# A four-layer hybrid backbone: start-up reordered around the modulation steps, and the latent half of x loaded and squared later

## The chip, the cores and the metric

The kernel runs on one core of one Trainium2 chip. The metric is the time of one execution on the device in microseconds (us), the median of several runs. A core has five engines that run their own instruction streams and wait for one another by semaphores: TensorE (PE; its weight loads are listed as PEld), VectorE (DVE), ScalarE (ACT), GpSimd (POOL) and SyncE (SP), which issues most of the transfers. TensorE's granted clock has two levels, 1.2 and 2.4 GHz; the profile gives it as a share of the higher one.

## What is computed

Four layers run over 512 tokens of 1024 features: 256 context tokens and 256 latent tokens. Each layer has a mixer (latent attention in layers 0 and 3, a convolution module in layer 1, a Hyena operator in layer 2) and a gated feed-forward part with a short convolution. Each mixer and feed-forward part sees a normed and modulated input. Cut to what this case touches, in the reference:

```python
def rmsnorm(x, g):
    xf = x.astype(F32)
    y = xf * lax.rsqrt(jnp.mean(xf * xf, axis=-1, keepdims=True) + EPS)
    return (y * g.astype(F32)).astype(x.dtype)

def modulate(x, g, shift, scale):
    return rmsnorm(x, g) * (1 + scale) + shift
...
    sh1, sc1, g1, sh2, sc2, g2 = jnp.split(s_lat @ ada_w[i] + ada_b[i], 6, axis=-1)
    csh1, csc1, cg1, csh2, csc2, cg2 = jnp.split(s_ctx @ ada_w[i] + ada_b[i], 6, axis=-1)
    hl = modulate(x, norm_mix[i], sh1, sc1)
...
    hdn = jnp.sin(fr * (z @ f_w1.astype(F32) + f_b1.astype(F32)))
    hdn = jnp.sin(fr * (hdn @ f_w2.astype(F32) + f_b2.astype(F32)))
    hf = hdn @ f_w3.astype(F32)
...
    k = jnp.concatenate([h_fwd, jnp.zeros((1, D_MODEL), F32), h_bwd[1:][::-1]], axis=0)
    return k / (jnp.sum(jnp.abs(k), axis=0, keepdims=True) + EPS)
```

The modulation vectors come from `c` and `c_ctx` alone, and the spectrum of the Hyena filter from weights alone. The kernel computes both while it starts up, before and between the first products of layer 0.

## The kernel before

Features lie on the 128 partitions, in eight k-tiles; tokens lie along the free dimension, context in columns 0 to 255 and latent in 256 to 511. An fp32 number is split into a high and a low part (a ScalarE copy gives `whi`, `hh` or `g`, a VectorE subtraction gives `wlo`, `hl` or the second `g`), and a product is three matmuls (`mm3`, lines 158 to 160; two loops of line 636 and 642 in the attention's compression). In the trace an fp32 matmul stands as two entries.

The order of TensorE's instructions is that of the program text (`tc.manual_schedule(engines={PE})`). The order on the other engines is made by a scheduler; each engine then runs its list strictly in order. Transfers are issued from SP, one after the other, and an issue waits until its buffer is free.

The start-up, at the end of the program (lines 1360 to 1391), puts these together by hand:

- `warm_up(n)` (line 218) issues `n` matmuls of `ones` and `ident` whose result nobody uses (`idle` in the profile).
- `fill` takes the next step of `ada_group` (line 230): one k-tile of the first modulation vectors, four matmuls (`ada`, line 243). After the eighth, ScalarE copies the result out (line 248), and `settle` (line 254) transposes it and VectorE adds the bias (`mod`, line 262).
- `piece` takes the next step of the Hyena filter's spectrum: `spectra` (two sine layers on VectorE and ScalarE, lines 1100 to 1107, with four products between, line 1151), then `spectra_half(0, ...)` (line 1161). That makes for two halves `t` two products with the decay window (lines 1171, 1173, 1174), sum and difference, their splits, and the sum of absolute values `asum`; then four columns of spectra products (`fcol`, six matmuls each, copied out by line 1195), two to a piece.
- `Sq` (line 325) squares x on ScalarE (line 335) and adds the squares up (line 337); here on VectorE and over all 512 columns, six additions. `sums` (line 353) sums over the partitions with matmuls against `ones` (line 357), and ScalarE, a power on GpSimd (line 195) and ScalarE (line 364) make the token scales; `spread` (line 366) spreads them over the partitions by a matmul. `apply` (line 370) makes `moda` from `mod`, then for eight k-tiles `e` (VectorE), `hh` (ScalarE) and `hl` (VectorE). `apply(0)` is for the context, `apply(1)` for the latent tokens.
- `mla` (line 581) loads the compression weights `w_c` in two pairs (each split in two), and multiplies: for the context eight k-steps of line 636, with `sums(1)` behind the fourth, and the low halves (line 642), with `apply(1)` (and so the second `spread`) behind the first eight of them; then the same for the latent tokens.

The same `spectra_half` runs once more with `hc` of 1, by the spare steps of layer 1's feed-forward part, some 880 to 960 us into the span.

Of the kernel before, what the change touches and what calls it, by code (L numbers as in the profile page):

```python
# [15 lines left out]
AF = mybir.ActivationFunctionType  # L16
ALU = mybir.AluOpType
AX = mybir.AxisListType

P = 128  # L20
D = 1024
KT = D // P
T = 512
L = 256
# [11 lines left out]
CW = QL + KVL + PE  # L36
# [20 lines left out]
def r(ap):  # L57
    return ap.bitcast(F32R)
# [25 lines left out]
def kernel(ctx: ExitStack, tc: tile.TileContext, xT, cT, cB, ada0, ada2, adaT1, adaT2, adaT3, prm, mlp, w_c, w_ug, w_o,  # L84
                         w_p1, w_p2, w_hi1, w_hi0, w_ho, w_fup, w_fd0, w_fd1, w_fd2, spec0, f_w3, decay, dft, c_dft, c_b, out,
                         layers=(0, 1, 2, 3), final=True):
# [18 lines left out]
    def e_tile(shape=None):  # L105
        return gp.tile(shape or [P, T], F32, tag="g", name="e")
# [55 lines left out]
    def both(t, f):  # L162
        return f(t[0]), f(t[1])

    def stt(o, a, s, b, op0, op1, **kw):
        nc.vector.scalar_tensor_tensor(out=o, in0=a, scalar=s, in1=b, op0=op0, op1=op1, **kw)  # L166

    def split(hi, lo, src):
        nc.scalar.activation(out=r(hi), in_=src, func=AF.Copy)  # L169
        nc.vector.tensor_tensor(out=r(lo), in0=src, in1=hi, op=ALU.subtract)  # L170

    def rsqrt_seed(eng, v, n, tag):
        y = sp.tile([P, n], F32, tag=tag + "y", name="rsy", bufs=2)
# [44 lines left out]
    def warm_up(n):  # L218
        idle = pm.tile([P, T], F32, tag="mm", name="idle")
        for i in range(n):  # L220
            nc.tensor.matmul(out=idle[:, 0:P], lhsT=ident, rhs=ones, start=True, stop=True)  # L221
# [8 lines left out]
    def ada_group(li, g, early=False):  # L230
        mod_tile(li)
        ps = pa.tile([P, T], F32, tag="ada", name="ada")
        for k in range(KT):
            if early and k in (2, 3, 4):
                raws = [wp.tile([P, 1024], F32, tag="w", name="aw", bufs=WB) for _ in range(2)]
            else:
                raws = [wp.tile([P, 2048], F32, tag="raw", name="raw", bufs=RAW)]
            n = 4 // len(raws)
            for i, raw in enumerate(raws):
                at = (4 * g + n * i) * T  # L240
                nc.sync.dma_start(out=raw, in_=(ada0, None, ada2)[li][k * P:(k + 1) * P, at:at + n * T])
            for c in range(4):
                nc.tensor.matmul(out=ps[32 * c:32 * c + 32, :], lhsT=spad[:, k, :], rhs=raws[c // n][:, c % n * T:(c % n + 1) * T],  # L243
                                 start=(k == 0), stop=(k == KT - 1))
            if k < KT - 1:
                yield
        sb = e_tile()
        nc.scalar.activation(out=sb, in_=ps, func=AF.Copy)
        late.append((li, g, sb))
        yield  # L250

    late = []

    def settle():
        if not late:
# [43 lines left out]
    def fill(n=1):  # L299
        for _ in range(n):  # L300
            settle()
            if units[0] < cap[0] and next(filler[0], 1) is None:
                units[0] += 1
# [14 lines left out]
    def need(n):  # L318
        while units[0] < n:
            was = units[0]  # L320
            fill()
            if units[0] == was:
                break

    class Sq:
        def __init__(self, c0, eng=nc.gpsimd):
            self.c0, self.acc, self.n, self.parts, self.eng = c0, None, [0, 0], {}, eng
# [18 lines left out]
    class Norm:  # L346
# [23 lines left out]
        def apply(self, s):  # L370
            if s not in self.R:
                self.spread(s)
            R = self.R[s]
            v = slice(s * L, (s + 1) * L)
            self.m = mods[self.li]
            if self.a is None:
                self.a = sp.tile([P, KT, 2], F32, tag="moda", name="moda")
                stt(self.a, self.m[:, self.c + 8:self.c + 16, :], 1.0, self.g.unsqueeze(2).to_broadcast([P, KT, 2]),
                    ALU.add, ALU.mult)
            hs = []  # L380
            shift = lambda k: self.m[:, self.c + k, s:s + 1]
            for k in range(KT):
                hs.append(e_tile()[:, v])
                stt(hs[k], x[:, k, v], self.a[:, k, s:s + 1], R[:, v], ALU.mult, ALU.mult)
                nc.scalar.activation(out=r(HH[:, k, v]), in_=hs[k], func=AF.Identity, bias=shift(k))
            with tc.high_priority(offset=-18 if s == 0 else 0):
                for k in range(KT):
                    stt(r(HL[:, k, v]), hs[k], shift(k), HH[:, k, v], ALU.add, ALU.subtract)
# [192 lines left out]
    def mla(li, nm):  # L581
# [4 lines left out]
        cps = [ps_mm() for _ in range(4)]  # L586
        w = []
        for u in range(2):
            w += [both(t, lambda a: a.rearrange("p (k c) -> p k c", k=2)) for t in load_w(w_c[j, u], 2 * CW, 2 * CW)]
        if li == layers[0]:  # L590
            spill()
        widths = ((0, QL), (QL, QL + KVL), (QL + KVL, CW))
# [568 lines left out]
    def spectra_half(hc, loaded):  # L1161
        w3, dec, raw = loaded
        fh, fl = [g_tile(), g_tile()], [g_tile(), g_tile()]
        for t in range(2):
            split(fh[t], fl[t], raw[:, t * T:(t + 1) * T])
        fwd = lambda t, a, b: (fh[t][:, a:b], fl[t][:, a:b])
        ab, asum = [], []
        for t in range(2):
            pf, pb = ps_mm(), ps_mm()
            for w, ps in ((0, pf), (1, pb)):  # L1170
                nc.tensor.matmul(out=ps, lhsT=h2[:, t * P:(t + 1) * P], rhs=w3[w][0:FO, :], start=True, stop=True)
            f, b, s, d = e_tile(), e_tile(), e_tile(), e_tile()
            nc.vector.tensor_tensor(out=f, in0=pf, in1=dec[t], op=ALU.mult)
            nc.vector.tensor_tensor(out=b, in0=pb, in1=dec[t], op=ALU.mult)
            if t == 0:
                nc.vector.memset(b[0:1, :], 0.0)
            nc.vector.tensor_tensor(out=s, in0=f, in1=b, op=ALU.add)
            nc.vector.tensor_tensor(out=d, in0=b, in1=f, op=ALU.subtract)
            hl4 = [g_tile() for _ in range(4)]
            split(hl4[0], hl4[1], s)  # L1180
            split(hl4[2], hl4[3], d)
            ab.append(((hl4[0], hl4[1]), (hl4[2], hl4[3])))
            stt(f, f, -1.0, f, ALU.mult, ALU.max)
            stt(b, b, -1.0, b, ALU.mult, ALU.max)
            nc.vector.tensor_tensor(out=f, in0=f, in1=b, op=ALU.add)
            asum.append(f)
            yield
        kf = [[e_tile(), e_tile()] for _ in range(2)]
        for fcol, w in ((0, 0), (1, 0), (2, 1), (3, 1)):
            ps = ps_mm()  # L1190
            for t in range(2):
                mm3(ps, fwd(t, fcol * P, (fcol + 1) * P), ab[t][w], t == 0, t == 1)
            f2, im = fcol % 2, fcol // 2
            for j in range(2):
                nc.scalar.activation(out=kf[j][f2][:, im * L:(im + 1) * L], in_=ps[:, j * L:(j + 1) * L], func=AF.Copy)
            if fcol % 2:
                yield
        ps = ps_mm()
        for t in range(2):
            mm3(ps[0:32, :], fwd(t, 2 * P, 2 * P + 32), ab[t][0], t == 0, t == 1)  # L1200
        for j in range(2):
            nc.scalar.activation(out=kf[j][0][0:1, L:T], in_=ps[0:1, j * L:(j + 1) * L], func=AF.Copy)
            for f2 in range(2):
                nc.sync.dma_start(out=kf_d[:, 2 * hc + j, f2 * T:(f2 + 1) * T], in_=kf[j][f2])
        nps = ps_tr()
        for c in range(4):
            for t in range(2):
                nc.tensor.matmul(out=nps[:, c:c + 1], lhsT=asum[t][:, c * P:(c + 1) * P], rhs=ones[:, 0:1],
                                 start=(t == 0), stop=(t == 1))
        v = slice(4 * hc, 4 * hc + 4)  # L1210
        nc.vector.tensor_scalar(out=rn[:, v], in0=nps[:, 0:4], scalar1=EPS, scalar2=None, op0=ALU.add)
        nc.vector.reciprocal(out=rn[:, v], in_=rn[:, v])
        yield
# [147 lines left out]

    with tc.manual_schedule(engines={mybir.EngineType.PE}):
        filler[0] = chain(ada_group(0, 0, True), ada_group(0, 1), ada_group(0, 2), ada_group(2, 0))
        la, lb = spectra_load()
        pieces = chain(spectra(la), spectra_half(0, lb))
        sq = Sq(0, nc.vector)
        nm = Norm(layers[0], 0, sq)
        def piece():
            kas.extend(next(pieces) or ())

        warm_up(WARM)
        fill(2)
        for k in (0, 4):
            nc.sync.dma_start(out=x[:, k:k + 4, :], in_=xT[:, k:k + 4, :])
        for k in range(KT):
            sq.add(k, 0, T)
        for i in range(3):
            piece()
        warm_up(12)
        fill()  # L1380
        for i in range(2):
            piece()
            warm_up(6)
            fill()
        nm.sums(0)
        fill(3)
        piece()
        settle()
        piece()
        nm.apply(0)  # L1390
        spare[0] = pieces

        for i, li in enumerate(layers):
            nm = (mla, conformer, hyena)[li % 3](li, nm)
            nm = ffn(li, nm)
# [164 lines left out]
```

## Time and profile before

| What | us |
|---|---|
| median of 3 runs | 2145.06 (2144.52 to 2145.59) |
| profiled execution, its own time | 2145.16 |
| its span, first to last instruction | 2143.3 |
| TensorE busy | 2096.1 (98%) |
| VectorE busy | 1557.3 (73%) |
| ScalarE busy | 1287.5 (60%) |
| GpSimd busy | 236.2 (11%) |

The mean granted clock of the span is 0.994. In the chain of work that ended last, 89% is TensorE, 4% VectorE, 3% ScalarE, 2% GpSimd, 1% transfers. The first fortieth of the span (0 to 54 us) is the one in which TensorE is busy 0.7 of the time; nearly all the others show 0.9 or more.

### The profile page before, as it was taken

To read this page: it belongs to the slowest core of one execution; us is meant where nothing else is said; L and a number is where in the kernel's file an instruction comes from. 1 tells how busy PE (TensorE), PEld (TensorE's weight loads), DVE (VectorE), ACT (ScalarE), POOL (GpSimd) and SP (SyncE) were. 2 spreads that over 40 slices of the span, in tenths; PEclk is the share of its full clock that TensorE was granted. 3 is DMA by queue.
4 is the path that set the end of the run, shared out by engine and by line. 5 is a ranking of instruction groups with operands and counts; after the bars stand their busy time and mean duration, and the time that the engine had idled before them with its cause. 6 is when DMAs were issued, how large, how long until landed. Compare 5 with 4: busy or idle time off the path is not lost.

```text
span 2143.3 us, 32063 instructions
## 1 busy us (share of the span) xinstructions
PE 2096.1 (98%) x12108; PEld 1801.3 (84%) x12108; DVE 1557.3 (73%) x2780; ACT 1287.5 (60%) x2774; POOL 236.2 (11%) x403
## 2 busy tenths in 40 slices
PE   7999999999999999999999999999999998899999
PEld 5767898888899979888888988898888888669999
DVE  5878368889756665768775689757979856976665
ACT  3788457778644465547654544456868745875453
POOL 0375200000020012000000200020000002621000
PEclk8999999999999999999999999999999999999999
DMA  8533135545432152444542322224545531114552
GB/s 316 211 131 139 60 118 179 214 177 200 173 128 84 59 205 81 155 150 163 196 171 85 114 85 93 99 79 158 210 182 196 197 113 50 58 46 171 180 189 85
DMA packets 48699, 305.39 MB, mean 142 GB/s; under 512 B 5536, under 2 KB 6688, under 8 KB 16160
## 3 DMA queue, kind: packets, MB, share of 16 engines
q1 hardware_dynamic: 47824, 300.91, 39.8%
q8 instruction: 95, 1.56, 0.3%
q10 hardware_dynamic: 720, 2.44, 0.3%
q14 instruction: 60, 0.49, 0.1%
HBM read 299.13 MB, written 4.19 MB: 142 GB/s over the span
## 4 chain that ended last, share of the span: by engine, by line
PE 89%; DVE 4%; ACT 3%; POOL 2%; DMA 1%; issue 1%; SPq 0%; POOLq 0%; ACTq 0%; DVEq 0%
PE mm L158 26%; PE mm L159 25%; PE mm L160 25%; PE mm L463 4%; PE mm L469 2%; PE mm L850 1%; PE ada L243 1%; PE tr L829 1%; PE mm L636 1%; ACT g L761 1%; DMA x<-in_xT_dram 1%; PE tr L357 1%; PE idle L221 1%; POOL e L337 1%; PE mm L642 0%
## 5 line engine op out<-in xcount | busy, mean ns | idle before, releaser
L158 PE MATMUL mm<-hh,whi 128*128 128x512 f32 (+1 forms) x1856 | 657.2, 354 | 0.0
L159 PE MATMUL mm<-hl,whi 128*128 128x512 f32 (+1 forms) x1856 | 654.5, 353 | 0.0
L160 PE MATMUL mm<-hh,wlo 128*128 128x512 f32 (+1 forms) x1856 | 654.2, 352 | 0.0
L147 DVE TENSOR_TENSOR wlo<-raw,whi 128x1024 fp32r<-128x1024 f32 (+2 forms) x361 | 430.0, 1193 | 290.4 <-PE mm L159 179.2
L144 ACT ACTIVATE whi<-raw 128x1024 fp32r<-128x1024 f32 (+3 forms) x370 | 374.6, 1017 | 293.9 <-PE mm L160 160.7
L158 PEld LDWEIGHTS mm<-hh,whi 128*128 128x128 f32 x1856 | 351.1, 189 | 51.7 <-issue 3.1
L160 PEld LDWEIGHTS mm<-hh,wlo 128*128 128x128 f32 x1856 | 351.0, 189 | 47.7
L159 PEld LDWEIGHTS mm<-hl,whi 128*128 128x128 f32 x1856 | 351.2, 189 | 46.3
L285 ACT ACTIVATE e<-e 128x512 f32<-128x512 f32 x512 | 315.9, 619 | 80.8 <-DVE e L284 80.5
L284 DVE TENSOR_TENSOR e<-raw,e 128x512 f32<-128x512 f32 x512 | 315.3, 684 | 0.0
L158 PE MATMUL mm<-g,whi 128*128 128x512 f32 (+1 forms) x904 | 309.1, 342 | 0.0
L159 PE MATMUL mm<-g,whi 128*128 128x512 f32 (+1 forms) x904 | 307.5, 340 | 0.0
L160 PE MATMUL mm<-g,wlo 128*128 128x512 f32 (+1 forms) x872 | 298.5, 342 | 0.0
L337 POOL TENSOR_TENSOR e<-e 128x256 f32<-128x256 f32 (+1 forms) x63 | 70.2, 1114 | 1209.7 <-ACT e L335 1176.6
L158 PEld LDWEIGHTS mm<-g,whi 128*128 128x128 f32 x904 | 171.3, 189 | 19.7
L159 PEld LDWEIGHTS mm<-g,whi 128*128 128x128 f32 x904 | 171.3, 190 | 19.6
L160 PEld LDWEIGHTS mm<-g,wlo 128*128 128x128 f32 x872 | 165.3, 190 | 19.0
L169 ACT ACTIVATE g<-e 128x512 fp32r<-128x512 f32 (+1 forms) x137 | 76.3, 558 | 106.4 <-DVE e L534 45.3
L166 DVE SCALAR_TENSOR_TENSOR e<-mm,par,e 128x510 f32<-128x510 f32 (+3 forms) x186 | 126.2, 678 | 15.6 <-ACT e L528 11.6
L166 DVE SCALAR_TENSOR_TENSOR x<-mm,mod,x 128x256 f32<-128x256 f32 x192 | 85.3, 477 | 52.0 <-PE mm L160 51.8
L170 DVE TENSOR_TENSOR g<-e,g 128x512 fp32r<-128x512 f32 (+1 forms) x137 | 81.9, 598 | 41.8 <-ACT g L169 41.4
L528 ACT ACTIVATE e<-mm,par 128x512 f32<-128x512 f32 (+1 forms) x88 | 63.0, 716 | 63.7 <-PE mm L160 59.2
(264 smaller groups left out, 2856.1 us busy)
## 6 DMA issues: line engine op xcount, KB each, us to landing
raw<-in_w_fup_dram SPq DMA_DIRECT2D x88, 1024.0 KB, 4.9
raw<-in_adaT_dram SPq DMA_DIRECT2D x64, 1024.0 KB, 4.8
raw<-in_w_fd_dram SPq DMA_DIRECT2D x32, 1024.0 KB, 4.9
raw<-in_ada_dram SPq DMA_DIRECT2D x29, 1024.0 KB, 5.2
raw<-in_w_fd_dram SPq DMA_DIRECT2D x16, 768.0 KB, 4.2
raw<-in_w_p_dram SPq DMA_DIRECT2D x12, 1024.0 KB, 4.9
raw<-in_w_hi_dram SPq DMA_DIRECT2D x12, 1024.0 KB, 5.0
raw<-in_w_o_dram SPq DMA_DIRECT2D x8, 1024.0 KB, 4.9
```

The source lines that it names most:

```text
L144: nc.scalar.activation(out=r(hi[:, 0:n]), in_=part, func=AF.Copy)
L147: nc.vector.tensor_tensor(out=r(lo[:, 0:n]), in0=part, in1=hi[:, 0:n], op=ALU.subtract)
L158: nc.tensor.matmul(out=ps, lhsT=r(ah), rhs=r(bh), start=start, stop=False)
L159: nc.tensor.matmul(out=ps, lhsT=r(ah), rhs=r(bl), start=False, stop=False)
L160: nc.tensor.matmul(out=ps, lhsT=r(al), rhs=r(bh), start=False, stop=stop)
L166: nc.vector.scalar_tensor_tensor(out=o, in0=a, scalar=s, in1=b, op0=op0, op1=op1, **kw)
L169: nc.scalar.activation(out=r(hi), in_=src, func=AF.Copy)
L170: nc.vector.tensor_tensor(out=r(lo), in0=src, in1=hi, op=ALU.subtract)
L284: nc.vector.tensor_tensor(out=t, in0=raw[:, q * D + (i % 2) * T:q * D + (i % 2 + 1) * T], in1=sb[i], op=ALU.mult)
L285: nc.scalar.activation(out=t, in_=t, func=AF.Copy, accum_out=asum[:, 2 * u + q, i // 2, i % 2:i % 2 + 1])
L337: self.eng.tensor_tensor(out=self.acc[:, a:b], in0=self.acc[:, a:b], in1=t[:, a:b], op=ALU.add)
L463: nc.tensor.matmul(out=banks[i][q][:, v], lhsT=r(wq[:, k, :]), rhs=r(HH[:, k, v]), start=k == 0 and wq is w[i][q][0], stop=False)
```

## The change

It has four parts.

1. **x in two column halves.** Two loads of four k-tiles over all columns become a load of the context columns in the same place, and a load of the latent columns behind the first `w_c` load. Each partition's piece is then 1 KB long where it was 8 KB.
2. **Squares and their additions.** `Sq` of layer 0 adds on GpSimd instead of VectorE, in 128x256 pieces: six additions for the context, six for the latent tokens. The context squares are issued in the program after the first half `t` of the spectra, the latent ones in `mla`, where `queued("apply")` makes the scheduler issue them after the eight `hh` copies of the context.
3. **Spectra.** In `spectra_half` the absolute values and their sums are issued after the splits of both halves (`queued("parts")`). For `hc` of 0 each column of spectra products is a piece of its own, and the modulation steps come singly between them. The idle matmuls in between go from 12, 6 and 6 to 10, 4 and 4, and the context's `spread` comes ahead of the last column.
4. **Weight splits.** The splits of the first `w_c` pair are issued after the copy-out of the modulation and after `moda`, those of the second pair after the eight `hh` copies.

The diff, without the lines that only return instructions so that they can be marked:

```diff
+    def queued(*names):
+        st = ExitStack()
+        for n in names:
+            st.enter_context(tc.issue_after(marks[n]))
+        return st
...
         for u in range(2):
-            w += [both(t, lambda a: a.rearrange("p (k c) -> p k c", k=2)) for t in load_w(w_c[j, u], 2 * CW, 2 * CW)]
+            with queued(*((("evict", "moda"), ("apply",))[u] if li == layers[0] else ())):
+                w += [both(t, lambda a: a.rearrange("p (k c) -> p k c", k=2)) for t in load_w(w_c[j, u], 2 * CW, 2 * CW)]
+            if li == layers[0] and u == 0:
+                load_x(1)
+                with queued("apply"):
+                    for k in range(KT):
+                        nm.sq.add(k, L, T)
...
             split(hl4[0], hl4[1], s)
-            split(hl4[2], hl4[3], d)
+            marks["parts"] = split(hl4[2], hl4[3], d).ins
             ab.append(((hl4[0], hl4[1]), (hl4[2], hl4[3])))
-            stt(f, f, -1.0, f, ALU.mult, ALU.max)
-            stt(b, b, -1.0, b, ALU.mult, ALU.max)
-            nc.vector.tensor_tensor(out=f, in0=f, in1=b, op=ALU.add)
-            asum.append(f)
+            fb.append((f, b))
             yield
+        with queued("parts"):
+            for f, b in fb:
+                stt(f, f, -1.0, f, ALU.mult, ALU.max)
+                stt(b, b, -1.0, b, ALU.mult, ALU.max)
+                nc.vector.tensor_tensor(out=f, in0=f, in1=b, op=ALU.add)
+                asum.append(f)
...
-            if fcol % 2:
+            if fcol % 2 or hc == 0:
                 yield
...
-        sq = Sq(0, nc.vector)
+        sq = Sq(0)
         nm = Norm(layers[0], 0, sq)
+
         def piece():
             kas.extend(next(pieces) or ())
 
+        def load_x(s):
+            nc.sync.dma_start(out=x[:, :, s * L:(s + 1) * L], in_=xT[:, :, s * L:(s + 1) * L])
+
         warm_up(WARM)
         fill(2)
-        for k in (0, 4):
-            nc.sync.dma_start(out=x[:, k:k + 4, :], in_=xT[:, k:k + 4, :])
-        for k in range(KT):
-            sq.add(k, 0, T)
+        load_x(0)
         for i in range(3):
             piece()
-        warm_up(12)
+        warm_up(10)
+        piece()
+        for k in range(KT):
+            sq.add(k, 0, L)
         fill()
-        for i in range(2):
-            piece()
-            warm_up(6)
-            fill()
+        piece()
+        warm_up(4)
+        fill(2)
+        piece()
+        fill()
+        piece()
+        fill()
         nm.sums(0)
-        fill(3)
         piece()
+        fill()
+        warm_up(4)
         settle()
+        nm.spread(0)
         piece()
         nm.apply(0)
```

In the order of the instructions the change shows at three places. The first is GpSimd, from the end of its constants to the first power of the attention's compression (`tv` is the mean square of a norm, `css` that of the compression; line numbers with a minus are of before, with a plus of the change).

```order
-L195 TENSOR_TENSOR rsy<-tv,nhalf 128x2 x2
-L611 TENSOR_SCALAR css<-css 128x6
+L345 TENSOR_TENSOR e<-e 128x256 x6
+L195 TENSOR_TENSOR rsy<-tv,nhalf 128x2
+L345 TENSOR_TENSOR e<-e 128x256 x6
+L195 TENSOR_TENSOR rsy<-tv,nhalf 128x2
+L627 TENSOR_SCALAR css<-css 128x6
```

Six additions now stand ahead of each of the two powers; before, GpSimd had none here.

The second is TensorE, from the transposes of the second sine layer to the sums of the context norm. Before:

```order
L1157 MATMUL tr<-e 64x256
L221 MATMUL idle<-ones,ident 128x128 x12
L243 MATMUL ada<-aw,spad 32x512 x4
L1171 MATMUL mm<-w_108,e 128x512 x2
L221 MATMUL idle<-ones,ident 128x128 x6
L243 MATMUL ada<-aw,spad 32x512 x4
L1171 MATMUL mm<-w_108,e 128x512 x2
L221 MATMUL idle<-ones,ident 128x128 x6
L243 MATMUL ada<-aw,spad 32x512 x4
L357 MATMUL tr<-ones,e 128x1 x4
```

With the change:

```order
L1173 MATMUL tr<-e 64x256
L221 MATMUL idle<-ones,ident 128x128 x10
L1187 MATMUL mm<-w_108,e 128x512 x2
L243 MATMUL ada<-aw,spad 32x512 x4
L1187 MATMUL mm<-w_108,e 128x512 x2
L221 MATMUL idle<-ones,ident 128x128 x4
L243 MATMUL ada<-aw,spad 32x512 x8
...
L243 MATMUL ada<-raw,spad 32x512 x4
L365 MATMUL tr<-ones,e 128x1 x4
```

The products of the first half `t` go ahead of the modulation step, and the sums (line 365, before 357) move behind two columns of spectra products and two more modulation steps.

The third is ScalarE around the context's `hh` copies. Before:

```order
L1195 ACTIVATE e<-mm 128x256 x2
L385 ACTIVATE hh<-e,mod 128x256 x7
L144 ACTIVATE whi<-raw 128x512
L385 ACTIVATE hh<-e,mod 128x256
L360 ACTIVATE tv<-tr,eps 128x2
L144 ACTIVATE whi<-raw 128x768
L364 ACTIVATE e<-ident,rsy 128x128 x2
```

With the change:

```order
L1214 ACTIVATE e<-mm 128x256 x2
L394 ACTIVATE hh<-e,mod 128x256 x8
L343 ACTIVATE e<-x 128x256 x8
L144 ACTIVATE whi<-raw 128x832
L368 ACTIVATE tv<-tr,eps 128x2
L144 ACTIVATE whi<-raw 128x832
L372 ACTIVATE e<-ident,rsy 128x128 x2
```

The eight latent squares (line 343) come behind the eight `hh` copies, and both high halves of the second weight pair (`whi`, 128x832) behind those, the second one behind the small copy `tv` of the latent norm.

## Rows read from the trace of the kernel before

**Rows 1.** Page, part 1: busy us (share) x instructions.

```profile
PE 2096.1 (98%) x12108; PEld 1801.3 (84%) x12108; DVE 1557.3 (73%) x2780; ACT 1287.5 (60%) x2774; POOL 236.2 (11%) x403
```

**Rows 2.** Waits, 880 to 980 us: who <- whom, us, times, longest.

```profile
PEld mm L1171 <- DVE e L166: 0.4, 1, 0.4
```

**Rows 3.** Chain that ended last, 0 to 84 us: start us, us, what.

```profile
32.21 1.91 PE mm L1171 x4
...
52.51 3.30 PE mm L636 x16
55.81 0.80 PE tr L357 x8
...
56.97 3.82 POOL rsy L195
60.82 0.70 ACT e L364 x2
61.56 0.70 PE mm L368 x2
```

**Rows 4.** Timeline, PE, 12 to 60 us: start us, us, instruction [idle before <- releaser].

```profile
13.31 3.69 PE L1151 MATMUL mm<-w,e 31*128 31x512 f32 x8
25.04 1.11 PE L1157 MATMUL tr<-e 64*64 64x256 f32 x2 [8.03 <-ACT e L1107]
26.08 5.14 PE L221 MATMUL idle<-ones,ident 128*128 128x128 f32 x24
```

**Rows 5.** Timeline, DVE, 12 to 62 us.

```profile
22.14 0.53 DVE L1100 TENSOR_SCALAR e<-tr,par 64x256 f32<-64x256 f32 x1
...
44.94 0.69 DVE L1185 TENSOR_TENSOR e<-e 128x512 f32<-128x512 f32 x1
...
48.45 0.17 DVE L166 SCALAR_TENSOR_TENSOR moda<-mod,par 128x16 f32<-128x16 f32 x1
49.26 1.96 DVE L147 TENSOR_TENSOR wlo<-raw,whi 128x832 fp32r<-128x832 f32 x2 [0.63 <-ACT whi L144]
51.43 3.22 DVE L166 SCALAR_TENSOR_TENSOR e<-x,moda,mm 128x256 f32<-128x256 f32 x8 [0.21 <-PE mm L368]
...
55.51 3.25 DVE L166 SCALAR_TENSOR_TENSOR hl<-e,mod,hh 128x256 fp32r<-128x256 f32 x8
```

**Rows 6.** Stretches: length; busy of PE, PEld, DVE, ACT, POOL; PEclk, DMA share, GB/s.

```profile
17.00:18.00 1.00, 0.01 (x1) 0.00 (x0) 0.89 (x2) 0.68 (x2) 0.00 (x0) 0.53 1.08 442
30.00:31.00 1.00, 1.00 (x8) 1.00 (x6) 0.88 (x2) 0.07 (x1) 0.00 (x0) 0.64 1.02 426
...
1828.00:1830.00 2.00, 0.00 (x0) 0.00 (x0) 2.00 (x9) 1.11 (x2) 1.50 (x7) 0.88 0.00 0
...
1832.00:1834.00 2.00, 0.77 (x3) 0.48 (x4) 2.00 (x11) 0.00 (x0) 0.41 (x1) 0.50 0.00 0
...
1836.00:1838.00 2.00, 1.48 (x9) 1.12 (x8) 1.21 (x4) 1.55 (x4) 1.50 (x7) 0.91 0.93 242
```

**Rows 7.** Instructions of lines 337, 195, 335: count, ns min/median/max, first and last start.

```profile
L337 POOL TENSOR_TENSOR e<-e x63: 726/742/5416, 239.1 to 1942.3; 128x256 f32<-128x256 f32 x48, 128x512 f32<-128x512 f32 x15
...
L195 POOL TENSOR_TENSOR rsy<-tv,nhalf x15: 707/717/3813, 42.5 to 1946.2; 128x2 f32<-128x2 f32 x15
...
L335 ACT ACTIVATE e<-x x92: 400/418/634, 15.5 to 1944.6; 128x256 f32<-128x256 f32 x64, 128x512 f32<-128x512 f32 x28
```

**Rows 8.** Timeline, POOL and DVE, 825 to 834 us.

```profile
827.94 5.42 POOL L337 TENSOR_TENSOR e<-e 128x256 f32<-128x256 f32 x1 [3.60 <-ACT e L335]
...
827.24 2.85 DVE L166 SCALAR_TENSOR_TENSOR hl<-e,mod,hh 128x256 fp32r<-128x256 f32 x7
830.01 0.48 DVE L166 SCALAR_TENSOR_TENSOR x<-e,mod,x 128x256 f32<-128x256 f32 x1
830.41 2.35 DVE L147 TENSOR_TENSOR wlo<-raw,whi 128x1024 fp32r<-128x1024 f32 x2
```

**Rows 9.** Timeline, ACT, 36 to 62 us.

```profile
44.92 0.60 ACT L248 ACTIVATE e<-ada 128x512 f32<-128x512 f32 x1
...
51.95 2.91 ACT L385 ACTIVATE hh<-e,mod 128x256 fp32r<-128x256 f32 x7
```

More of the change, by code (lines that the diff above doesn't have):

```diff
@@ L165, in stt @@
     def stt(o, a, s, b, op0, op1, **kw):
-        nc.vector.scalar_tensor_tensor(out=o, in0=a, scalar=s, in1=b, op0=op0, op1=op1, **kw)
+        return nc.vector.scalar_tensor_tensor(out=o, in0=a, scalar=s, in1=b, op0=op0, op1=op1, **kw)
     def split(hi, lo, src):
         nc.scalar.activation(out=r(hi), in_=src, func=AF.Copy)
-        nc.vector.tensor_tensor(out=r(lo), in0=src, in1=hi, op=ALU.subtract)
+        return nc.vector.tensor_tensor(out=r(lo), in0=src, in1=hi, op=ALU.subtract)
     def rsqrt_seed(eng, v, n, tag):
@@ L247, in ada_group @@
         sb = e_tile()
-        nc.scalar.activation(out=sb, in_=ps, func=AF.Copy)
+        evict = nc.scalar.activation(out=sb, in_=ps, func=AF.Copy)
         late.append((li, g, sb))
+        if (li, g) == (0, 0):
+            marks["evict"] = evict.ins
         yield
-    late = []
+    late, marks = [], {}
     def settle():
@@ L377, in apply @@
                 self.a = sp.tile([P, KT, 2], F32, tag="moda", name="moda")
-                stt(self.a, self.m[:, self.c + 8:self.c + 16, :], 1.0, self.g.unsqueeze(2).to_broadcast([P, KT, 2]),
-                    ALU.add, ALU.mult)
+                a = stt(self.a, self.m[:, self.c + 8:self.c + 16, :], 1.0, self.g.unsqueeze(2).to_broadcast([P, KT, 2]),
+                        ALU.add, ALU.mult)
+                marks.setdefault("moda", a.ins)
             hs = []
@@ L384, in apply @@
                 stt(hs[k], x[:, k, v], self.a[:, k, s:s + 1], R[:, v], ALU.mult, ALU.mult)
-                nc.scalar.activation(out=r(HH[:, k, v]), in_=hs[k], func=AF.Identity, bias=shift(k))
+                hi = nc.scalar.activation(out=r(HH[:, k, v]), in_=hs[k], func=AF.Identity, bias=shift(k))
+            marks.setdefault("apply", hi.ins)
             with tc.high_priority(offset=-18 if s == 0 else 0):
@@ L1166, in spectra_half @@
         fwd = lambda t, a, b: (fh[t][:, a:b], fl[t][:, a:b])
-        ab, asum = [], []
+        ab, asum, fb = [], [], []
         for t in range(2):
```

## Prediction

> **What bounds the kernel now.** I read the page first. TensorE is busy for nearly the whole span [rows 1], so time can change only where it waits or where its clock is low. The edit touches two places: the first 80 us, and one spectra half among the matmuls of layer 1. The waits of that second place are short: the longest that a spectra product has there on VectorE is 0.4 us [rows 2]. Moving VectorE work there later by some 2 us changes nothing I can find a price for, so I cost that part at nothing; the cover is the dense feed-forward matmuls, and if it failed the loss would be of the order of that 0.4 us.
>
> So the sum is one of the start-up, read in the chain of waits [rows 3]. VectorE first adds the squares of x (until 22.2), then does the first sine layer, and only then can TensorE make the second sine's transposes at 25.04, after 8.03 us of idling [rows 4]. From there idle matmuls, modulation steps and spectra products lead to the first context product at 52.51, whose release was ScalarE's `hh` copy. After 16 of them come the sums of the latent norm (55.81), a power on GpSimd that takes 3.82 us, the second spread (61.56), and the rest.
>
> **What the change removes.** The six 128x512 additions leave VectorE [rows 5]: the sine layer that now starts at 22.14 can start at 13.4, when its matmuls are done. It takes 2.4 us on VectorE and 0.42 on ScalarE, so it ends at 16.2, before TensorE comes out of the products of line 1151 (13.31 + 3.69 = 17.0 [rows 4]). The second transposes go to 17.0 from 25.04: 8.0 us earlier. The second sine took 4.0 us from those transposes to its result; it ends at 21.0.
>
> **The clock on this stretch.** The granted clock fell just after 17.0, when the matmuls stopped, and returned inside the slice from 30 to 31 [rows 6], whose mean of 0.64 puts the return at 30.7, that is 4.6 us after the idle matmuls began at 26.08 [rows 4]. In a later stretch of the same trace TensorE resumed in the slice from 1832 to 1834 (0.77 us busy of it, so at about 1832.9 with its gaps) and the clock rose at about 1836.3, 3.4 us on. After the change full-array matmuls resume at 18.1, 20 trace entries instead of 24, so the return is at 21.5 to 22.7. 24 entries took 5.14 us at mostly half level, so 20 take up to 4.3 us, until 22.4 at the latest. I put the first spectra product at 21.6, against 32.21 before.
>
> **Spectra to the first norm.** Before, it took from 32.21 to 44.94 (the start of the last sum of absolute values) until both halves were split: 12.7 us. Three instructions at a pitch of 0.6 (1.8 us) now stand behind, so splits end at 21.6 + 10.9, about 32.4, and the six instructions for the absolute values at 32.4 + 6 x 0.63 = 36.2.
>
> The **context additions** are the operation that the trace of before has nowhere in this place: six GpSimd additions of 128x256 beside a busy VectorE. Alone one takes 0.74 us [rows 7]. But the one that began at 827.94 took 5.42, and VectorE ran seven `hl`, an `x` and two `wlo`, without a pause from 827.24 to 832.8 [rows 8]; the GpSimd work ended just after it. The 3.82 us power at 56.97 likewise ended with the VectorE run (60.2). So the bounds of one addition are 0.74 us and "until VectorE pauses", and I take the second, since those two rows are the nearest in operands and engine. The seven `hh` copies in 2.91 us follow each other at 0.40, about 0.09 less than one lasts [rows 9]; squares of 0.42 us [rows 7] so follow at 0.33, and eight of them end at 30; three additions fit in VectorE's pauses until 30.8, three come after 36.2: 36.2 + 3 x 0.79 = 38.5. The sums take 0.95 us: 39.4. With a small copy (0.3), a power of 0.72 when nothing holds it [rows 7] and two copies (0.70 [rows 3]) the spread is ready at 41.2; as TensorE stands in the sums until 39.4, one spectra column (6 x 0.23) and the last modulation step (1.0) end at 41.9.
>
> The Trainium skill speaks against my choice ("SBUF — State Buffer", section "SBUF: two separate sides"): the pair shared by VectorE and GpSimd is an exclusive lock held for a whole instruction, and whoever starts first blocks the other until it ends. By it an addition would wait for at most one VectorE instruction, and the sum would be that of rival B, below. This case's trace does not agree: 5.42 us across some ten VectorE instructions.
>
> **Modulation to the first context product.** Eviction 0.6 [rows 9] (42.5), idle matmuls and transposes 0.9, `mod` and `moda` 0.5: 43.9, against 48.62 before [rows 5]. One `wlo` (0.94) now goes ahead of the `e` products: the first at 44.8, against 51.43. ScalarE still has two copies of the last spectra column ahead of `hh`, the first of which is done at 46.7, where the first context product starts: 5.8 us earlier than 52.51. Sixteen entries of the context matmuls take 3.3 us; the low half of the second weight pair adds 0.1: 50.1 to 50.3.
>
> **The latent squares** now stand behind the eight `hh` copies. These end at 46.2 + 8 x 0.4 = 49.4; eight squares x 0.33 end at 52.05. VectorE's `hl` run (3.25 us for eight [rows 5]) lies at 48.9 to 52.1 and holds GpSimd. Six dependent additions then take 6 x 0.79 = 4.7 us, and one `wlo` of 0.9 gets in between: 57.6. TensorE has them in order behind its fourth context step, so it waits 7.3 us; nothing else is queued that it may do. The sums end at 58.6, against 56.46: **2.1 us later**. That gives back the 5.8 and more: before, TensorE went from the fourth context step into the same sums without a wait [rows 3]. The next 16 context entries take 3.1 us, and 0.5 more for the second weight load, whose high half now sits behind the small copy of the norm on ScalarE: 62.2. After 1.5 us of low-half products the spread comes at 63.7, against 61.56, also 2.1 later. (Before, TensorE waited 0.65 us there for the slow power; that wait goes, the power lying in an empty VectorE stretch.) What follows keeps its order.
>
> **The clock again.** TensorE idle for 7.3 us: in the trace it idled from about 1826.5 to 1832.9, and the slices of 1828 to 1830 and 1832 to 1834 show 0.88 and 0.50 [rows 6]. So here it falls at about 53.4 and comes back 3.4 us after 57.6. Half level for 3.4 us costs at most 1.7 us, some of it inside the later wait for weights: 1.3, with ends 0 and 3.1 (a return as late as 4.6 us on, and a second stretch).
>
> **The transfers** I cost at nothing. x in two column halves has pieces of 1 KB where it had 8 KB. The queue moved 426 GB/s in the slice at 30 [rows 6]; at that rate half of x (1 MB) takes 2.5 us, at half of it 5. Context x is squared from 27 on, latent x (issued behind the first context weights, some 35 us) from 49: 9 us of cover even then. What stands behind x on the queue, the modulation weights, lands 2.5 us earlier; the second context weight pair still waits for a buffer, as it did before, and its split is the 0.5 above.
>
> **Sum:** +2.1 + 1.3 = +3.4 us on the profiled execution's 2145.16, so **2148.6**; that execution stands 0.1 over the median of the runs shown. A measurement of this kernel can tell 0.2%, 4.3 us, from no change; 3.4 is inside.
>
> **Rivals.** *A, slower:* the clock does not return in the first stretch until the splits and the modulation steps are past. In its favour: before, the clock rose at 30.7 while idle matmuls were still running (until 31.2); here they end by 22.4, before the later of the two returns (22.7), and what follows are small products with gaps. Against: the other stretch had its clock back 3.4 us after TensorE resumed. If it returns at 24 the end moves by 1.65 us more, at 27 by 2.9, and the drop at the latent sums lasts as long again: +5 to +7, **2151**. It is beyond 0.2% as soon as the return is later than about 23.
>
> *B, faster:* GpSimd is not held for more than one VectorE instruction. Then context sums end at 36, the context products start at 43.4 to 44, the latent additions end one step behind the squares (51.3 to 52.9), and the spread comes 2.5 to 4.0 us earlier than before: 2141.1 to 2142.7, **2142**. For it: an addition of 0.74 is the median of 63 [rows 7]. Against: 5.42 and 3.82.
>
> *C, half of each:* the additions of one half are held and the others slip in. Context alone held: TensorE's sums wait only till the squares (52.5), and the spread comes 2 us earlier: 2143. Latent alone held: 3.5 us gained in the first half, 3.4 lost: 2145. A middle of **2145**.
>
> *D, nothing moves:* the chain behind the second sine turns out to rest on the weights' landing or on ScalarE, and the change hides: **2145**.
>
> **The numbers.** Forecast 0.42 (its own range 2146.7 to 2150), A 0.20, C 0.20, B 0.12, D 0.06. Slower by over 0.2% (above 2149.5): nearly all of A and a fifth of the forecast, 0.27. Faster (below 2140.9): the edge of B and what I may have missed in the same direction, 0.09. Within: 0.64. The range runs from the middle of B to the upper part of A: 2142.0 to 2151.5.
>
> **What would show it.** The first VectorE sine instruction at 13.4; transposes at 17.0; first context product near 46.7; six GpSimd additions of which one or two last over 2 us; latent sums starting near 57.6 with 7 us of TensorE idle ahead of them and a clock of 0.5 behind; the spread near 64 to 65. It would be wrong if GpSimd's additions stayed near 0.8 us beside VectorE runs (then B), or if the clock row of 22 to 27 stays at 0.5 (then A).

## The result, and the profile after

The changed kernel takes 2159.6 us (median of 4 runs, 2157.98 to 2159.95) against 2144.8 for the kernel before: a ratio of 1.0067, 95% interval 1.0051 to 1.0083. The forecast was 2148.6 in a range up to 2151.5. It is slower by 14.8 us where 3.4 were forecast.

The profiled execution took 2159.42 us, with a span of 2157.6 against 2143.3. The page's busy line:

```profile
PE 2105.0 (98%) x12096; PEld 1804.6 (84%) x12096; DVE 1555.3 (72%) x2774; ACT 1288.3 (60%) x2782; POOL 245.0 (11%) x415
```

TensorE is busy 8.9 us longer than in [rows 1] with no more instructions: part of the time is a low clock.

To see where the 14.3 us arise, I followed VectorE's additions into x (`x<-mm,mod,x`), which TensorE's products release, through both traces. At 236 us in the kernel before they are 4.1 us late, at 944 us 5.7, at 1083 us 14.3, and it stays 14.3 to the end. The pair at 1083, first the kernel before:

```profile
1083.28 1.65 DVE L166 SCALAR_TENSOR_TENSOR x<-mm,mod,x 128x256 f32<-128x256 f32 x4
1097.57 1.65 DVE L166 SCALAR_TENSOR_TENSOR x<-mm,mod,x 128x256 f32<-128x256 f32 x4
```

So there are three pieces: **4.1 us in the start-up, 1.6 near 775 us, 8.6 between 983 and 1083 us**, in layer 1's feed-forward part. Only the first was in the forecast.

**The start-up** came out near the forecast. The chain that ended last, 14 to 80 us (start, us, what), which answers to [rows 3]:

```profile
17.95 1.04 PE tr L1173 x2
...
45.53 3.19 ACT hh L394 x8
48.72 0.62 ACT e L343 x2
...
52.29 1.39 POOL e L345
53.76 0.72 POOL e L345
...
56.94 1.86 PE tr L365 x8
58.80 5.50 PE mm L652 x16
64.31 1.50 PE mm L658 x8
65.81 0.43 PE mm L376 x2
```

The second transposes come at 17.9 instead of 25.04, the first context product at 46.0 instead of 52.51. Then the eight latent squares (line 343) follow the eight `hh` copies, GpSimd's additions follow them, and TensorE waits for these. The sums start at 56.94 instead of 55.81, and the spread of the latent half at 65.81 instead of 61.56. The wait, in the timeline of TensorE from 56 us on:

```profile
56.94 1.86 PE L365 MATMUL tr<-ones,e 128*128 128x1 f32 x8 [6.83 <-POOL e L345]
```

The stretches of the start-up (length; busy of PE, PEld, DVE, ACT, POOL; granted clock, DMA share, GB/s):

```profile
16.00:18.00 2.00, 2.00 (x4) 0.42 (x3) 0.00 (x0) 1.81 (x5) 0.00 (x0) 0.53 1.07 407
22.00:24.00 2.00, 2.00 (x10) 1.60 (x9) 1.29 (x2) 0.92 (x2) 0.00 (x0) 0.77 1.02 410
52.00:54.00 2.00, 0.00 (x0) 0.00 (x0) 1.09 (x1) 0.00 (x0) 1.84 (x3) 0.91 0.28 119
54.00:56.00 2.00, 0.00 (x0) 0.00 (x0) 0.00 (x0) 0.00 (x0) 1.84 (x3) 0.50 0.00 0
62.00:64.00 2.00, 2.00 (x8) 1.92 (x7) 0.86 (x1) 0.00 (x0) 0.00 (x0) 0.53 1.07 321
```

The clock falls at about 53.6 and is back only at about 63.9, so the sums (1.86 us against 0.80 before in the chain) and the second half of the context products (5.50 us, against 3.3 for the first half in [rows 3]) run at the lower level, 1.2 GHz.

**Layer 1's feed-forward part** is what the forecast left out. There TensorE, which in the kernel before is busy 5.00 of every 5 us from 985 to 1005, stops. One of these stretches before:

```profile
995.00:1000.00 5.00, 5.00 (x24) 4.14 (x23) 5.00 (x8) 3.81 (x11) 0.00 (x0) 1.00 0.64 229
```

The same view of the changed kernel:

```profile
990.00:995.00 5.00, 5.00 (x24) 4.14 (x23) 5.00 (x9) 5.00 (x18) 0.00 (x0) 1.00 0.65 215
995.00:1000.00 5.00, 0.45 (x2) 0.02 (x1) 5.00 (x9) 5.00 (x16) 0.00 (x0) 0.91 0.69 218
1000.00:1005.00 5.00, 3.41 (x7) 2.30 (x8) 4.84 (x7) 4.65 (x8) 0.00 (x0) 0.50 0.50 200
1005.00:1010.00 5.00, 5.00 (x21) 4.03 (x21) 5.00 (x8) 2.92 (x8) 0.00 (x0) 0.90 0.90 292
```

Its waits there (who waited for whom, us, times, longest):

```profile
PE mm L158 <- ACT whi L144: 6.1, 1, 6.1
```

TensorE waits 6.1 us for the high half of an up-projection weight, and the clock falls to half level behind that: the nine matmuls from 1001.55 to 1005.97 take 4.4 us where nine take 2.0 at the high level. The two together, 8.5 us, make up the 8.6 of this piece. VectorE and ScalarE are busy all the while. With what? ScalarE first (the timeline just ahead of that copy):

```profile
998.57 0.76 ACT L538 ACTIVATE e<-mm,par 128x512 f32<-128x512 f32 x1
999.23 0.62 ACT L287 ACTIVATE e<-e 128x512 f32<-128x512 f32 x1
...
999.85 0.62 ACT L287 ACTIVATE e<-e 128x512 f32<-128x512 f32 x1
1000.37 0.19 ACT L287 ACTIVATION_READ_ACCUMULATOR e<-e 128x1 f32 x1
1000.46 1.04 ACT L144 ACTIVATE whi<-raw 128x1024 fp32r<-128x1024 f32 x1
```

Line 287 is ScalarE's half of `ada_side`: the modulation vectors of a later layer are made beside the feed-forward part, by a product on VectorE (line 286) and a sum on ScalarE for each of eight pieces of a unit. Nobody needs them soon. The `whi` copy stands in ScalarE's list behind them; its weight had landed at 994.0, so the transfer did not hold it. And on VectorE, 970 to 1002 us:

```profile
976.45 0.48 DVE L166 SCALAR_TENSOR_TENSOR x<-mm,mod,x 128x256 f32<-128x256 f32 x1 [4.56 <-PE mm L160]
976.90 0.69 DVE L170 TENSOR_TENSOR g<-e,g 128x512 fp32r<-128x512 f32 x1
977.51 0.48 DVE L166 SCALAR_TENSOR_TENSOR x<-mm,mod,x 128x256 f32<-128x256 f32 x1
977.90 0.68 DVE L170 TENSOR_TENSOR g<-e,g 128x512 fp32r<-128x512 f32 x1
978.50 0.69 DVE L166 SCALAR_TENSOR_TENSOR e<-e 128x512 f32<-128x512 f32 x1
...
981.02 0.69 DVE L1205 TENSOR_TENSOR e<-e 128x512 f32<-128x512 f32 x1
...
984.28 14.53 DVE L286 TENSOR_TENSOR e<-raw,e 128x512 f32<-128x512 f32 x24
```

The same place in the kernel before:

```profile
970.83 0.87 DVE L166 SCALAR_TENSOR_TENSOR x<-mm,mod,x 128x256 f32<-128x256 f32 x2 [4.56 <-PE mm L160]
971.94 0.69 DVE L170 TENSOR_TENSOR g<-e,g 128x512 fp32r<-128x512 f32 x1 [0.24 <-PE mm L159]
972.55 9.12 DVE L284 TENSOR_TENSOR e<-raw,e 128x512 f32<-128x512 f32 x15
```

Before, the side products start at 972.55, right behind the x that TensorE released. Now the two last splits of the second spectra half, four of the six instructions for its absolute values (lines 166 and 1205) and the arithmetic of a feed-forward unit (line 544 and its neighbours) stand between them and that x. They start at 984.28. The kernel runs 5.7 us late at this point, so without the change they would have started at 972.55 + 5.7 = 978.3: they are 6.0 us late.

That alone would cost nearly nothing. In the kernel before, ScalarE makes this `whi` copy behind 15 of the sums:

```profile
981.91 0.62 ACT L285 ACTIVATE e<-e 128x512 f32<-128x512 f32 x1
...
982.64 1.06 ACT L144 ACTIVATE whi<-raw 128x1024 fp32r<-128x1024 f32 x1
983.61 0.61 ACT L285 ACTIVATE e<-e 128x512 f32<-128x512 f32 x1
```

Now it stands behind all 24 and one more instruction of the feed-forward unit (line 538), and starts at 1000.46: 12.1 us later than 982.64 + 5.7. At its old place it would have ended at 983.70 + 5.7 = 989.4, and TensorE stopped at 995.4, so there was a slack of 6.0 us. The later start of the side products uses up that slack; the nine further sums (0.61 us each) and the 0.7 us of line 538 are TensorE's wait of 6.1.

### The profile page after: what moved, and what is told of

The parts are those of the page before. It is cut to its first block, busy times and chain, and to the rows that moved or that the text cites. A ratio compares the mean times of both kernels' runs of the same rounds, so it can differ in the third digit from the quotient of the medians.

```text
span 2157.6 us, 32065 instructions
## 1 busy us (share of the span) xinstructions
PE 2105.0 (98%) x12096; PEld 1804.6 (84%) x12096; DVE 1555.3 (72%) x2774; ACT 1288.3 (60%) x2782; POOL 245.0 (11%) x415
## 4 chain that ended last, share of the span: by engine, by line
PE 88%; DVE 4%; ACT 4%; POOL 2%; issue 1%; DMA 1%; SPq 0%; POOLq 0%; ACTq 0%; DVEq 0%
PE mm L158 25%; PE mm L159 25%; PE mm L160 25%; PE mm L473 4%; PE mm L479 2%; PE mm L866 1%; PE mm L652 1%; PE ada L243 1%; PE tr L845 1%; POOL e L345 1%; ACT g L777 1%; PE tr L365 1%; ACT hh L394 1%; PE mm L658 1%; DMA raw<-in_ada_dram 0%
## 5 line engine op out<-in xcount | busy, mean ns | idle before, releaser
L345 POOL TENSOR_TENSOR e<-e 128x256 f32<-128x256 f32 (+1 forms) x75 | 83.0, 1106 | 1255.9 <-ACT e L343 1254.3
L166 DVE SCALAR_TENSOR_TENSOR e<-mm,par,e 128x510 f32<-128x510 f32 (+3 forms) x186 | 126.2, 678 | 14.3 <-ACT e L538 10.4
```

Source lines behind the costliest of these rows:

```text
L166: return nc.vector.scalar_tensor_tensor(out=o, in0=a, scalar=s, in1=b, op0=op0, op1=op1, **kw)
L345: self.eng.tensor_tensor(out=self.acc[:, a:b], in0=self.acc[:, a:b], in1=t[:, a:b], op=ALU.add)
```

## Experiments

Part 3 of the change has the edge `queued("parts")` in `spectra_half`: it binds the absolute values behind the last split, also in the second call, in layer 1, where the pieces lie two feed-forward units apart. Theory: this edge is the 8.6 us, and the start-up is the rest. Rival: the start-up's shift moved transfers and clock phases, and these made the stall.

### ffn_edge_off: the change without the edge in layer 1

```diff
             ab.append(((hl4[0], hl4[1]), (hl4[2], hl4[3])))
-            fb.append((f, b))
+            if hc:
+                stt(f, f, -1.0, f, ALU.mult, ALU.max)
+                stt(b, b, -1.0, b, ALU.mult, ALU.max)
+                nc.vector.tensor_tensor(out=f, in0=f, in1=b, op=ALU.add)
+                asum.append(f)
+            else:
+                fb.append((f, b))
             yield
```

Expected: 

> The changed kernel, with the absolute values of the second spectra half (hc of 1, layer 1) back inline. Theory (the extra time is two separate things: +4.1 us at the start-up, and some 8.6 us in the feed-forward part of layer 1, where that edge reorders VectorE and ScalarE): 2159.6 - 8.6 = 2151, no TensorE idle of 6 us near 995, lag to the kernel before of 4 us at 500 us and 4 to 6 at the end. Rival (the stall near 995 comes from the later start-up, by shifting transfers and clock phases): 2158 to 2160, with the stall still there.

Measured: 2151.13 us (2148.61 to 2153.11), ratio 1.0023 (1.0013 to 1.0032) to the kernel before at 2145.45 in these runs. TensorE no longer stops in layer 1; its stretch from 995 to 1000 us reads:

```profile
995.00:1000.00 5.00, 5.00 (x24) 4.14 (x23) 4.30 (x6) 3.14 (x5) 0.00 (x0) 1.00 0.72 252
```

8.5 us of the changed kernel's 2159.6 are gone (9.4 by the two ratios). What is left, 4.9 us by the ratio (2.8 to 6.9), is mostly the start-up that the forecast spoke of, at 3.4.

The lag was expected at 4 us at 500 us and at 4 to 6 at the end. In the profiled execution, the shortest of the ten (2148.61), it is 1.9 at 236 us, 1.8 at 513 and 3.5 at 1083. There the clock fell later in the start-up, at about 17.4, and the chain reads:

```profile
13.13 3.62 PE mm L1167 x8
...
63.79 0.43 PE mm L376 x2
```

The products of line 1167 took 4.48 us in the changed kernel's chain, and its spread came at 65.81. The two executions are 2 us apart here, most of it by when the clock fell.

### ffn_edge_only: the kernel before, with the edge in layer 1 alone

```diff
-            stt(f, f, -1.0, f, ALU.mult, ALU.max)
-            stt(b, b, -1.0, b, ALU.mult, ALU.max)
-            nc.vector.tensor_tensor(out=f, in0=f, in1=b, op=ALU.add)
-            asum.append(f)
+            if hc:
+                fb.append((f, b))
+            else:
...
             yield
+        if hc:
+            with tc.issue_after(parts[0]):
+                for f, b in fb:
...
```

Expected: 

> The kernel before, with only the absolute values of the second spectra half issued behind the splits of both halves (the start-up as before). Theory: 2144.8 + 8.6 = 2153.4, a TensorE wait of about 6 us for ScalarE's whi near 990 and a clock at half level behind it. Rival (the stall comes from the start-up's shift): 2144 to 2146.

Measured: 2154.95 us (2152.39 to 2155.18), ratio 1.0036 (1.0023 to 1.0049). The stall is there without any change to the start-up, in TensorE's timeline:

```profile
997.62 0.80 PE L158 MATMUL mm<-hh,whi 128*128 128x512 f32 x1 [6.11 <-ACT whi L144]
```

The rival falls: the edge alone makes the stall, 7.7 us by the ratio (4.9 to 10.5), and it is made by nothing else (ffn_edge_off).

### late_no_edge: the same place in the text, without the edge

```diff
-            with tc.issue_after(parts[0]):
+            if True:
```

(against ffn_edge_only). Expected: 

> The kernel before, with the absolute values of the second spectra half later in the program text, as in the run ffn_edge_only, but without the edge that binds them behind the last split. Theory (it is the edge that moves the 24 side products and the weight split, not the place in the text): 2144 to 2146. Rival (the place is enough): 2153.

Measured: 2145.96 us (2144.24 to 2148.84), ratio 1.0001 (0.9992 to 1.0011). The place in the program text is harmless. Without the edge the scheduler puts the absolute values of each half where they were, give or take two places; with it, they come 40 us and more later, just ahead of the 24 side products and behind them. Why the scheduler pulls the two last splits and a feed-forward unit along as well is not shown by these runs (the tiles that the first half keeps longer would be a reason).

### idle_filled: idle matmuls in the wait ahead of the latent sums

```diff
                 if s == 0 and k == 3:
+                    if li == layers[0]:
+                        warm_up(28)
                     nm.sums(1)
```

(on ffn_edge_off). Expected: 

> As ffn_edge_off, with 28 idle matmuls in TensorE's 7 us wait ahead of the latent sums. It prices the clock that falls there and stays low from 53.8 to 64.1. Theory (the clock is 3 to 3.5 us of the start-up's loss): 3 us less than ffn_edge_off, so about 2148, the spread near 62.5 instead of 65.8. Rival (the low clock lies beside waits for weights and power): within 1 us of ffn_edge_off.

Measured: 2149.04 us (2148.41 to 2151.46), 2.1 less than ffn_edge_off. TensorE's timeline:

```profile
50.01 6.41 PE L221 MATMUL idle<-ones,ident 128*128 128x128 f32 x56
...
58.62 1.05 PE L365 MATMUL tr<-ones,e 128*128 128x1 f32 x8 [2.19 <-POOL e L345]
```

The clock now falls for 3.4 us (60.2 to 63.6 by its stretches) instead of 10.2, and the sums take 1.05 us instead of 1.86. But the six GpSimd additions lasted 9.09 us here instead of 7.47, beside more VectorE work, so the sums began 1.7 us later than in the changed kernel. The spread came at 65.69 in this timeline, where 62.5 was expected; in the changed kernel's it is at 65.65. The test is not clean: in the profiled execution the later sums took back all that the clock gave. The medians differ by 2.1 us (1.3 by the ratios), but the times of the two kernels overlap, so the run does not settle what the clock costs.

### latent_on_dve: the latent additions on VectorE

```diff
                 load_x(1)
+                nm.sq.eng = nc.vector
                 with queued("apply"):
```

(on ffn_edge_off). Expected: 

> As ffn_edge_off, with the six latent additions on VectorE, the squares still behind the eight hh copies. Theory (of TensorE's 7 us wait some 2.5 us are additions held by the hl run, the rest is the place of the squares): the latent sums at about 54 instead of 55 to 57, a wait of 4 to 5 us left, 2 to 3 us less than ffn_edge_off, 2148. Rival (GpSimd being held is all of it): no wait, 2143.

Measured: 2147.68 us (2146.39 to 2149.05), ratio 1.0002 (0.9993 to 1.0012). The sums in TensorE's timeline:

```profile
54.33 1.84 PE L365 MATMUL tr<-ones,e 128*128 128x1 f32 x8 [4.12 <-DVE e L345]
```

As the theory had it: 2.6 us earlier than in the changed kernel, a wait of 4.1 us left, and a clock that still falls. GpSimd being held beside VectorE is less than half of the wait; the changed kernel's trace says the same, its first two latent additions lasting 2.80 and 1.39 us where the later ones take 0.73: 2.7 us more in all. What is left is the place of the squares and of the additions together: on VectorE the additions stand among the `hl` and `wlo` instructions, and the last ends at 54.2, 2.9 us behind the last square.

### latent_early: the latent squares ahead of the context norm

```diff
-            if li == layers[0] and u == 0:
-                load_x(1)
-                with queued("apply"):
-                    for k in range(KT):
-                        nm.sq.add(k, L, T)
...
         fill(2)
+        load_x(1)
         piece()
         fill()
+        sq.held = []
+        for k in range(KT):
+            sq.add(k, L, T)
         piece()
         fill()
         nm.sums(0)
+        with queued("pow"):
+            for t, a, b in sq.held:
+                nc.gpsimd.tensor_tensor(out=sq.acc[:, a:b], in0=sq.acc[:, a:b], in1=t[:, a:b], op=ALU.add)
+        sq.held = None
```

(on ffn_edge_off; `Sq.add` keeps its additions in `held` where that is a list, and `pow` marks the context's power.) Expected: 

> As ffn_edge_off, but the latent half of x is issued ahead of the last three modulation loads, its squares stand on ScalarE before the sums of the context norm, and its six GpSimd additions right behind the context's power, so that they are over before the hl run. Theory (the start-up's loss is the latent squares behind the eight hh copies, and what it brings: a wait of 7 us and a low clock): no wait ahead of the latent sums, no low clock between 50 and 65, the spread near 57 to 58 against 61.6 before, 4 us less than the kernel before, about 2141. Rival (GpSimd beside VectorE is slow wherever it lies): sums still late, 2148 or more.

Measured: 2142.07 us (2140.43 to 2143.09), ratio 0.9981 (0.9971 to 0.9991): **faster than the kernel before**, by 4.1 us (1.9 to 6.2), and 9.1 less than ffn_edge_off. Against the change as it was made it is some 17 less, 8.5 of them by the edge. The load, the squares and the additions were moved together; what each is worth was not tried. GpSimd in this kernel, 10 to 68 us:

```profile
30.84 6.12 POOL L348 TENSOR_TENSOR e<-e 128x256 f32<-128x256 f32 x6 [29.00 <-ACT e L344]
40.95 0.71 POOL L195 TENSOR_TENSOR rsy<-tv,nhalf 128x2 f32<-128x2 f32 x1 [3.99 <-ACT tv L371]
41.63 5.46 POOL L1422 TENSOR_TENSOR e<-e 128x256 f32<-128x256 f32 x6
```

The additions are over at 47.1, before VectorE's `hl` run, and the sums follow the fourth context step with no wait; TensorE and its clock (PEclk, the third number from the end) in the next stretch:

```profile
50.00:55.00 5.00, 4.36 (x26) 4.33 (x27) 5.00 (x10) 3.39 (x8) 0.81 (x1) 1.00 0.65 225
```

The spread comes at 57.67, 3.9 us before [rows 3] although the chip's clock in this execution was at its low level for 10.2 us near 20, longer than in the changed kernel.

## Why the prediction was wrong

The start-up was forecast step by step, and its total held, in part by luck (below). The step that failed is the first paragraph's: "Moving VectorE work there later by some 2 us changes nothing I can find a price for, so I cost that part at nothing; the cover is the dense feed-forward matmuls". The loss that it allowed for, should the cover fail, was 0.4 us. In its place stand 8.5 us. The row it rested on [rows 2] tells what a spectra product waits for with the old order. It says nothing of the weight copies on ScalarE, and nothing of an order that a scheduler makes anew when an edge is added. The price is not in the six moved instructions but in the 24 products of 0.6 us: they start 6.0 us later, which uses up the slack of a weight copy, and nine more of their sums pass ahead of that copy. This could be read without a chip: the two orders of VectorE and ScalarE differ by whole blocks in that part, and I compared only the start-up's.

Point by point:

- **Second transposes at 17.0:** 17.88. The clock fell while the products of line 1167 ran, at about 16.1 and not after them, and these took 4.55 us instead of 3.69. In the profiled execution of ffn_edge_off it fell behind them, and the transposes came at 16.68.
- **Clock back at 21.5 to 22.7, first spectra product at 21.6:** back at about 22.9, product at 23.25, 1.65 us late. Rival A (back after 23) did not happen; in the forecast's favour by little. In ffn_edge_off: back at 20.8, product at 21.31. The row of that return was read a little late: TensorE resumed at 1832.45 there, not 1832.9, so the clock came 3.9 us later and not 3.4.
- **Context additions held until VectorE pauses, the last ending at 38.5:** wrong in the mechanism. Here rival B and the second case of rival C had it. All six ran from 29.29 to 35.41, one every 1.02 us, and VectorE's instructions beside them grew (below). The sums stood behind other TensorE work until 37.97, close to the 38.4 forecast for their start.
- **First context product at 46.7:** 45.98, by luck: the spectra came 1.65 us later than forecast, and what follows them was 2.4 us shorter. In ffn_edge_off, where the clock came back in time, it is at 44.06, near the 43.4 to 44 of rival B.
- **Latent sums at 57.6 after a wait of 7.3 us:** 56.94 after 6.83. The first latent addition was held by the `hl` run as forecast.
- **The clock, 1.3 us:** the term of the sum that was mis-sized in the start-up. It was low for 10.2 us, 6.9 of them after TensorE resumed, where the row I took it from showed 3.4. With 1.86 us for the sums instead of 0.95 and 5.50 for the next context products instead of the 3.6 worked out (3.1 and 0.5 of waiting for weights) it costs 2.8 us. As the sums were 0.7 us early, the spread came at 65.81 where 65.0 was forecast with the clock.
- **Start-up in all, +3.4:** 4.0 in the profile at the end of the latent products, 4.9 (2.8 to 6.9) by the runs of ffn_edge_off. The 4.9 are inside the range, with errors of both signs in them.
- **The 1.6 us near 775**, in no part of the forecast, came from the clock, low for 3.4 us there (773.8 to 777.3). TensorE had been busy since 766; it had two waits of 0.8 and 0.9 us before that, and the kernel before has the same two without a low clock. Why it fell stays open. It comes without the change too: the profiled execution of late_no_edge, which has the old start-up, shows a low clock near 772 (its stretch from 770 to 775 us: 0.50), and its span is 3.4 us longer than that of the kernel before.

## What to carry to other kernels

An edge or a mark that orders a few instructions must be costed wherever the function that holds it is called, and in a scheduled kernel the cost is the new order of everything near it: compare both orders on every engine that it touches, for the whole program, before pricing anything at nothing. Work that nobody needs soon (here, side products) is dangerous in an in-order queue when it slips ahead of a split that the critical engine needs.

In a start-up, bringing one chain forward by 7 us gains nothing if the next link was moved behind it: put the second half's preparation (here squares and sums) into the first chain's waits, and not behind its last step.

## What the runs showed of the hardware

GpSimd and VectorE, both with two SBUF inputs, met in two ways. Beside VectorE's 128x512 instructions they alternated. The two timelines of the changed kernel, first GpSimd, around 33 us:

```profile
32.08 2.19 POOL L345 TENSOR_TENSOR e<-e 128x256 f32<-128x256 f32 x2
```

and VectorE, 32 to 33 us:

```profile
31.32 1.23 DVE L1194 TENSOR_TENSOR e<-e 128x512 f32<-128x512 f32 x1
32.47 1.21 DVE L170 TENSOR_TENSOR g<-e,g 128x512 fp32r<-128x512 f32 x1
```

An addition took 1.06 us instead of 0.73, and a VectorE instruction 1.2 instead of 0.69, one of each every 1.13 us: as if each waited for one of the other's. That is the rule of the Trainium skill ("SBUF — State Buffer", section "SBUF: two separate sides"), the lock held for one instruction, and here the trace agrees with it. Beside the run of eight 128x256 `hl` instructions, which follow each other at 0.40 us, the first latent addition took 2.80 us:

```profile
49.41 2.80 POOL L345 TENSOR_TENSOR e<-e 128x256 f32<-128x256 f32 x1 [9.30 <-ACT e L343]
```

It began among them and ended at 52.2, 0.6 us after the run did (51.63), so it waited for five or six instructions. By that rule, as the prediction read it, it would have waited for one; here the trace does not agree. What tells the two cases apart was not tried. In the first, VectorE's instructions depended on each other or on ScalarE, and GpSimd was already at work when they came; in the second VectorE was first.

The length of a low-clock stretch was not the same from one to the next: 3.4 us (idle_filled, near 62), 6.8 (the changed kernel, 16.1 to 22.9) and 10.2 (its wait for the latent sums). One row of such a stretch is no price for another. Nor did the clock of the start-up fall at one time: at about 17.4 us in the profiled execution of ffn_edge_off, 16.1 in that of the changed kernel and 14.6 in that of latent_early, behind the same instructions of TensorE. The four products between the two sine layers (line 1167, in latent_early 1165; eight instructions in the trace) took 3.69, 4.55 and 5.91 us.
